# Attention with unnormalized probabilities: the sums of a pair inverted together and multiplied into the gate

## The chip, the core and the metric

The kernel runs on one core of a Trainium2 chip. The metric is the device time of one execution in microseconds. It is launched as one program, and its inputs and outputs lie in the chip's memory (DRAM here).

## What is computed

A trunk of two layers for 2048 frames of 1024 channels. Layer A is a gated mixing layer with a spatial gate. Layer B is attention in chunks of 64 frames: each chunk sees itself and the eight chunks before it. Only layer B matters here:

```python
q, z = jnp.split(h @ w_qz, 2, axis=-1)              # 16 heads of 64 channels
sc = jnp.einsum('bqhd,bkhd->bhqk', qc, kc) + bias   # relative-position bias
sc = jnp.where(valid, sc, NEG_INF)
p = jax.nn.softmax(sc, axis=-1)
o = jnp.einsum('bhqk,bkhd->bqhd', p, vc)
...
return (o * jax.nn.silu(z)) @ w_out
```

The softmax divides each row of exponentials by its sum. That division is linear in each row, so it can stand before the product with the values or after it.

## The kernel before, in words

All products are made in a split form: each matrix is held as a high part and a low part, and three matmuls (lines 113 to 115) give one product. Layer A and the values of layer B come first. The attention starts at about 1560 us and is one long loop, written out at build time.

**The loop.** The frames are cut into four blocks t of 512, and the 16 heads into eight pairs p. A pair holds eight units u: two heads times four groups of 128 queries. One pass of the loop (lines 1633 to 1669) works on one unit of one pair and interleaves several things:

- `score` for the unit two places ahead. PE multiplies queries and keys (L1320), 640 keys for a group. DVE adds the bias, negates, and finds the row minimum (L1328). ACT takes the exponential and sums each row into `sl` (L1335). DVE inverts that sum (L1338), and POOL multiplies the 128x640 probabilities `pr` by it (L1339).
- `flip` for this unit. PE transposes the five 128x128 squares of `pr` into PSUM (L1359). There is one such buffer, `tp`. ACT copies the high part out (L1362) and DVE makes the low part (L1363).
- `value` at every second unit. PE multiplies transposed probabilities and values for two groups (L1380 to L1387). ACT and DVE bring the result into `og32` (L1399 to L1406). At a pair's last group, which is reached at unit 0 of the next pair, DVE multiplies `og32` by 0.5 and the gate `Z` (L1413), and SP stores the product in DRAM (L1418) for the output projection. In the last block the pairs 6 and 7 skip the DRAM: `last_og` multiplies into the place where the output projection reads (L1486), and POOL makes the sums that it needs.
- Between these stand steps of other work (`ahead`): the projections of the next pair (matmuls `pj`) to queries, keys and the gate `Z`, and the output projection of the block before (matmuls `bo`). `SHARE` says how many steps of it each pair takes. In the last block's last pair little is left to fill in, and the last output projection follows behind the loop.

**Weights.** Each projection loads its weights (L208 or L210), ACT casts them to the high part (L199), and DVE makes the low part (L200). In block t=0 they are raw, so POOL scales them first (L184) and SP stores the scaled ones (L212) for the later blocks. In t=0, pairs 2 and 4 also make combinations of the output weights (`o_sums`).

**Queues and order.** Every DMA is issued by SP, in order: a DMA whose data or place isn't ready holds those behind it. Each engine also works in order. The tile framework lays out the order of each engine ahead of time from its own estimates, under the dependencies and some ordering edges (`paced_by_pj`), so it isn't strictly that of the source.

**What the change touches.** `score` (L1305), `flip` (L1344), the end of `value` (L1409 to L1418), the loop body (L1646 to L1666) and the end (L1670). The tile `og` (two buffers) and the gate `Z` (two buffers) get new users.

Of the kernel before, what the change touches and what calls it, by code (L numbers as in the profile page):

```python
# [9 lines left out]
F32 = mybir.dt.float32  # L10
# [3 lines left out]
ALU = mybir.AluOpType  # L14
# [19 lines left out]
def trunk_kernel(  # L34
# [41 lines left out]
    xtd = [[dram.tile([P, D], F32, name=f"xtd{t}_{b}") for b in range(TB)] for t in range(NT)]  # L76
    ogd = [dram.tile([P, 2, NPAIR, 2, P], F32, name=f"ogd{t}") for t in range(NT)]
    x2d = [[dram.tile([P, D], F32, name=f"x2d{t}_{b}") for b in range(TB)] for t in range(NT - 1)]

    reld = [dram.tile([P * 768], F32, name=f"reld{h}") for h in range(NH)]  # L80

# [1125 lines left out]
    with ExitStack() as bctx:  # L1207
# [81 lines left out]
        ogt = {}  # L1289
        bias_t = {}  # L1290
        prs = {}
        pts = {}
        og32s = {}

# [10 lines left out]
        def score(t, p, u):  # L1305

            hd, qb = divmod(u, 4)
            h = 2 * p + hd
            if qb == 1 and (h + 1 < NH or t + 1 < NT):
                load_bias(t + (h + 1) // NH, (h + 1) % NH)  # L1310
            bias = bias_t[t, h]
            kx = kt[t, p, hd]
            c0 = 0 if t > 0 else 512 - qb * P
            n = 640 - c0
            koff = qb * P + c0
            ps = pss.tile([P, 2, 512], F32, tag="ss", name=f"s{t}_{h}_{qb}")
            nseg, w = (2, 320) if n == 640 else (1, n)
            for i, q in enumerate(qt[t, p, hd]):
                for sg in range(nseg):
                    mm(  # L1320
                        ps[:, sg, :w], q[:, qb * P : (qb + 1) * P],
                        kx[:, koff + sg * w : koff + (sg + 1) * w],
                        start=i == 0, stop=i == 1,
                    )
            pr = sb.tile([P, 640], F32, tag="Pr", name=f"pr{t}_{h}_{qb}", bufs=4)
            nm = sm.tile([P, 1], F32, tag="nm", name=f"nm{t}_{h}_{qb}", bufs=4)
            sl = sm.tile([P, 1], F32, tag="sl", name=f"sl{t}_{h}_{qb}", bufs=4)
            nc.vector.tensor_tensor_reduce(  # L1328
                out=pr[:, c0:].rearrange("p (a b) -> p a b", a=nseg),
                in0=ps[:, :nseg, :w],  # L1330
                in1=bias[:, c0:].rearrange("p (a b) -> p a b", a=nseg),
                scale=-1.0, scalar=3.0e38, op0=ALU.add, op1=ALU.min,
                accum_out=nm[:],
            )
            nc.scalar.activation(  # L1335
                pr[:, c0:], pr[:, c0:], AF.Exp, scale=-1.0, bias=nm[:], accum_out=sl[:]
            )
            nc.vector.reciprocal(sl[:], sl[:])  # L1338
            nc.gpsimd.tensor_scalar(  # L1339
                pr[:, c0:], pr[:, c0:], sl[:], 1.0, op0=ALU.mult, op1=ALU.mult  # L1340
            )
            prs[t, h, qb] = pr

        def flip(t, p, u):  # L1344

            hd, qb = divmod(u, 4)
            h = 2 * p + hd
            g, qq = divmod(qb, 2)
            if qq == 0:
                pt = sb.tile([P, 2, 6, 256], F32R, tag="PT", name=f"pt{t}_{h}_{g}", bufs=2)  # L1350
                if t == 0:
                    nc.gpsimd.memset(pt[:, :, 5, 0:P].bitcast(F32), 0.0)
                pts[t, h, g] = pt
            pt = pts[t, h, g]
            pr = prs[t, h, qb]
            b0 = 0 if t > 0 else 4 - qb
            tp = ptr.tile([P, KD, P], F32, tag="tr", name=f"tp{t}_{h}_{qb}")
            for b in range(b0, 5):
                tpose(tp[:, b, :], pr[:, b * P : (b + 1) * P], ident[:])  # L1359
            cs = slice(qq * P, (qq + 1) * P)  # L1360
            oh = pt[:, 0, b0 + qq : 5 + qq, cs]
            nc.scalar.copy(oh, tp[:, b0:5, :])  # L1362
            nc.vector.tensor_tensor(  # L1363
                pt[:, 1, b0 + qq : 5 + qq, cs], tp[:, b0:5, :], oh.bitcast(F32), op=ALU.subtract
            )

        def value(t, p, hd, g):

            h = 2 * p + hd
            pt = pts[t, h, g]  # L1370
            po = pmm.tile([P, 2, 256], F32, tag="mm", name=f"pv{t}_{h}_{g}")
            hs = slice(hd * P, hd * P + P)

            def keys(i):
                return vtl[t, p][:, 2 * g + i, hs]

            if t > 0:
                mm(po[:, :, 0:P], keys(0), pt[:, :, 0, 0:P], start=True, stop=False)  # L1380
                mm(po[:, :, P:256], keys(5), pt[:, :, 5, P:256], start=False, stop=False)
                blocks = range(1, 5)
            else:
                blocks = range(4 - 2 * g, 6)
            for j in range(2):
                for i in blocks:
                    mm(  # L1387
                        po[:, 0, :], keys(i), pt[:, j, i, :],
                        start=(t == 0 and j == 0 and i == blocks[0]),
                        stop=(j == 1 and i == blocks[-1]),  # L1390
                    )
            if hd == 0 and g == 0:
                og32s[t, p] = sb.tile([P, T], F32, tag="og32", name=f"og32_{t}_{p}", bufs=1)
            og32 = og32s[t, p]
            r, r2 = halves(hd)
            ot = sb.tile([P, 2, 256], F32, tag="ot", name=f"ot{t}_{h}_{g}", bufs=1)
            oq = og32[r, g * 256 : (g + 1) * 256]
            n = 2 if t > 0 else 1
            nc.scalar.copy(ot[r, :n, :], po[r2, :n, :])  # L1399
            o1 = ot[r, :, :] if t > 0 else oq  # L1400
            nc.vector.tensor_tensor(
                o1, po[r, :n, :] if t > 0 else po[r, 0, :],
                ot[r, :n, :] if t > 0 else ot[r, 0, :], op=ALU.add,
            )
            if t > 0:
                nc.vector.tensor_tensor(oq, ot[r, 0, :], ot[r, 1, :], op=ALU.add)  # L1406
            if g == 0:
                return
            if hd == 1 and t + 1 == NT and p >= 6:  # L1409
                last_og(p, og32, zt[t, p])  # L1410
            elif hd == 1:
                og = sb.tile([P, T], F32, tag="og", name=f"og{t}_{p}", bufs=2)
                nc.vector.scalar_tensor_tensor(  # L1413
                    og[:], og32[:], 0.5, zt[t, p][:], op0=ALU.mult, op1=ALU.mult
                )
                o4 = og[:].rearrange("p (j r s) -> p r j s", j=2, r=2)
                for r_ in range(2):
                    nc.sync.dma_start(ogd[t][:, r_, p], o4[:, r_])  # L1418
# [214 lines left out]
        for t in range(NT):  # L1633
            for p in range(NPAIR):
# [11 lines left out]
                for u in range(8):  # L1646
# [9 lines left out]
                        finals.pop(0)()  # L1656
                    if todo:
                        todo.pop(0)()
                    if u % 2 == 0:
                        if u:  # L1660
                            value(t, p, *divmod(u // 2 - 1, 2))
# [6 lines left out]
                    run(gen)  # L1668
                before = t, p
        value(*before, 1, 1)  # L1670
        run(gen)
        while finals:
            finals.pop(0)()
# [58 lines left out]
```

## Time and profile before

| what | us |
|---|---|
| median of 3 runs (2724.27 to 2734.33) | 2726.85 |
| profiled execution | 2731.61 |
| its span | 2728.6 |
| PE matmul busy | 2630.1 |
| DVE busy | 1961.0 |
| ACT busy | 1324.8 |
| POOL busy | 909.8 |

The profile is one execution. PE is TensorE's matmuls and PEld its weight loads, which overlap them; DVE is VectorE, ACT ScalarE, POOL GpSimd, SP SyncE. A group row gives line, engine, operation, what it writes and reads, and its count; then busy time and the mean of one in ns; then the idle time just before it and what ended that. A wait row reads "who waited, for whom: us in total, times, longest". Busy matmuls overlap each other in the records: what PE spends on one is read from the distance between two starts.

### The profile page before, as it was taken

The numbers are of one execution on the slowest core, as the hardware profiler recorded it, in microseconds if no ns is written. First come the engines' busy times: TensorE is split into PE (matmuls) and PEld (weight loads), VectorE is DVE, ScalarE is ACT, GpSimd is POOL, SyncE is SP. The second block draws the span as 40 slices with busy tenths as digits, with TensorE's granted clock in tenths as the row PEclk, the third lists the DMA queues.
The fourth block names the chain that finished last, engine by engine and source line by source line (L and its number), as shares of the span: only waits on it lengthen the run. The fifth ranks groups of instructions, "written<-read, shape, count | busy, mean of one in ns | idle before, by whom it ended". The sixth has DMA issues, their size and how long they took to land. (4 is left out here: it accounts for less than half of the span.)

```text
span 2728.6 us, 38857 instructions
## 1 busy us (share of the span) xinstructions
PE 2630.1 (96%) x13216; PEld 2199.9 (81%) x13216; DVE 1961.0 (72%) x3097; ACT 1324.8 (49%) x2360; POOL 909.8 (33%) x906
## 2 busy tenths in 40 slices
PE   8999999999999999999989998999999999999997
PEld 7888888888888888888867776778887888788885
DVE  5655676676676669666677776677788778877787
ACT  5422242433424445332455465566656666666554
POOL 3512236142251414115143344322333223323243
PEclk9999999999999999999999999899999999999999
DMA  7899999989888879668667787766777667865567
GB/s 297 314 326 335 345 358 327 329 306 349 333 300 295 302 263 342 236 236 308 239 219 277 238 274 249 243 211 208 234 253 246 219 211 238 264 203 192 185 228 251
DMA packets 274773, 735.56 MB, mean 270 GB/s; under 512 B 29584, under 2 KB 61328, under 8 KB 274576
## 3 DMA queue, kind: packets, MB, share of 16 engines
q1 hardware_dynamic: 274576, 733.09, 77.9%
q8 instruction: 105, 1.72, 0.3%
q14 instruction: 92, 0.75, 0.1%
HBM read 540.56 MB, written 181.93 MB: 265 GB/s over the span
## 5 line engine op out<-in xcount | busy, mean ns | idle before, releaser
L113 PE MATMUL P<-T,S 128*128 128x512 f32 x1248 | 496.1, 398 | 2.7 <-ACT S L376 2.0
L115 PE MATMUL P<-T,S 128*128 128x512 f32 x1248 | 490.3, 393 | 0.0
L114 PE MATMUL P<-T,S 128*128 128x512 f32 x1248 | 489.1, 392 | 1.1 <-DVE T L379 1.1
L1339 POOL TENSOR_SCALAR pr<-pr,sl 128x640 f32<-128x640 f32 (+4 forms) x256 | 202.8, 792 | 553.9 <-DVE sl L1338 512.8
L113 PE MATMUL pj<-hh_b,wh_b 128*128 128x512 f32 x768 | 316.8, 412 | 7.7 <-ACT wh_b L199 6.7
L114 PE MATMUL pj<-hl_b,wh_b 128*128 128x512 f32 x768 | 307.4, 400 | 0.0
L115 PE MATMUL pj<-hh_b,wl_b 128*128 128x512 f32 x768 | 306.5, 399 | 0.0
L1335 ACT ACTIVATE pr<-pr,nm 128x640 f32<-128x640 f32 (+4 forms) x256 | 195.3, 763 | 222.4 <-DVE nm L1328 217.5
L115 PEld LDWEIGHTS P<-T,S 128*128 128x128 f32 x1248 | 235.4, 189 | 50.3
L113 PEld LDWEIGHTS P<-T,S 128*128 128x128 f32 x1248 | 235.9, 189 | 48.1 <-ACT S L376 2.3
L114 PEld LDWEIGHTS P<-T,S 128*128 128x128 f32 x1248 | 235.8, 189 | 46.9 <-DVE T L379 1.3
L1363 DVE TENSOR_TENSOR pt<-tp,pt 128x640 fp32r<-128x640 f32 (+4 forms) x256 | 188.8, 738 | 75.4 <-ACT pt L1362 73.1
L1328 DVE CUSTOM_DVE_ANT_0 pr<-s,bias 128x640 f32<-128x640 f32 (+4 forms) x256 | 188.2, 735 | 21.4 <-PE s L1320 15.6
L1362 ACT CAST pt<-tp 128x640 fp32r<-128x640 f32 (+4 forms) x256 | 158.6, 620 | 60.8 <-PE tp L1359 58.0
L1359 PEld LDWEIGHTS tp<-ident,pr 128*128 128x128 f32 x1120 | 135.1, 140 | 54.5 <-POOL pr L1339 15.9
L1359 PE MATMUL tp<-ident,pr 128*128 128x128 f32 x1120 | 165.8, 274 | 12.7 <-DVE pt L1363 6.5
L115 PEld LDWEIGHTS pj<-hh_b,wl_b 128*128 128x128 f32 x768 | 147.3, 192 | 32.6
L113 PEld LDWEIGHTS pj<-hh_b,wh_b 128*128 128x128 f32 x768 | 147.7, 192 | 27.5 <-ACT wh_b L199 8.3
L114 PEld LDWEIGHTS pj<-hl_b,wh_b 128*128 128x128 f32 x768 | 147.9, 193 | 17.3 <-issue 0.2
L1387 PE MATMUL pv<-pt,V 128*128 128x256 f32 x960 | 143.0, 289 | 11.2 <-ACT pt L1362 11.1
L200 DVE TENSOR_TENSOR wl_b<-raw_b,wh_b 128x1024 fp32r<-128x1024 f32 x96 | 122.9, 1280 | 42.4 <-ACT wh_b L199 41.2
L1387 PEld LDWEIGHTS pv<-pt,V 128*128 128x128 f32 x960 | 127.5, 193 | 14.9 <-ACT pt L1362 13.6
(291 smaller groups left out, 5941.5 us busy)
## 6 DMA issues: line engine op xcount, KB each, us to landing
S<-hsd SPq DMA_DIRECT2D x288, 512.0 KB, 5.5
rw<-in_w_a SPq DMA_DIRECT2D x108, 512.0 KB, 6.5
A<-ytd SPq DMA_DIRECT2D x72, 512.0 KB, 5.5
raw_b<-wk SPq DMA_DIRECT2D x72, 512.0 KB, 3.8
hsd<-S SPq DMA_DIRECT2D x56, 512.0 KB, 4.3
V<-vhd SPq DMA_DIRECT2D x56, 512.0 KB, 5.0
wh_bo<-ows SPq DMA_DIRECT2D x50, 512.0 KB, 4.5
wl_bo<-ows SPq DMA_DIRECT2D x50, 512.0 KB, 5.6
```

The source lines that it names most:

```text
L113: first = mm(ps, lh, rh, start=first, stop=False)
L114: mm(ps, lh, rl, start=False, stop=False)
L115: mm(ps, ll, rh, start=False, stop=last)
L200: tv(wl[:], raw[:], wh[:].bitcast(F32), op=sub)
L1328: nc.vector.tensor_tensor_reduce(out=pr[:, c0:].rearrange("p (a b) -> p a b", a=nseg), in0=ps[:, :nseg, :w], in1=bias[:, c0:].rearrange("p ...
L1335: nc.scalar.activation(pr[:, c0:], pr[:, c0:], AF.Exp, scale=-1.0, bias=nm[:], accum_out=sl[:])
L1339: nc.gpsimd.tensor_scalar(pr[:, c0:], pr[:, c0:], sl[:], 1.0, op0=ALU.mult, op1=ALU.mult)
L1359: tpose(tp[:, b, :], pr[:, b * P : (b + 1) * P], ident[:])
L1362: nc.scalar.copy(oh, tp[:, b0:5, :])
L1363: nc.vector.tensor_tensor(pt[:, 1, b0 + qq : 5 + qq, cs], tp[:, b0:5, :], oh.bitcast(F32), op=ALU.subtract)
L1387: mm(po[:, 0, :], keys(i), pt[:, j, i, :], start=(t == 0 and j == 0 and i == blocks[0]), stop=(j == 1 and i == blocks[-1]),)
```

## The change

The probabilities stay unnormalized: the reciprocal and POOL's multiplication for each unit go. The row sums of a pair's eight units are collected as the eight columns of one tile. At unit 6 (unit 5 in the very last pair) PE transposes that tile into a free place of the `tp` buffer, DVE inverts the 8x128 result, SP stores it in DRAM as a row, and SP loads it back so that each head's 512 reciprocals stand on 64 partitions. POOL multiplies this tile by the gate. The product with the output moves from unit 0 to unit 1 of the next pair and reads the new tile instead of `Z`.

```diff
+    rcd = [dram.tile([NPAIR, 8 * P], F32, name=f"rcd{t}") for t in range(NT)]
...
-            sl = sm.tile([P, 1], F32, tag="sl", name=f"sl{t}_{h}_{qb}", bufs=4)
+            if u == 0:
+                sums[t, p] = sm.tile([P, 8], F32, tag="sl", name=f"sl{t}_{p}", bufs=2)
...
-                pr[:, c0:], pr[:, c0:], AF.Exp, scale=-1.0, bias=nm[:], accum_out=sl[:]
-            )
-            nc.vector.reciprocal(sl[:], sl[:])
-            nc.gpsimd.tensor_scalar(
-                pr[:, c0:], pr[:, c0:], sl[:], 1.0, op0=ALU.mult, op1=ALU.mult
+                pr[:, c0:], pr[:, c0:], AF.Exp, scale=-1.0, bias=nm[:],
+                accum_out=sums[t, p][:, u : u + 1],
             )
...
+            if u == sums_at(t, p):
+                tpose(tp[0:8, 5, :], sums[t, p][:], ident[:])
...
+            if u == sums_at(t, p):
+                inverse(t, p, tp[0:8, 5, :])
+
+        def sums_at(t, p):
+            return 5 if t + 1 == NT and p + 1 == NPAIR else 6
+
+        def inverse(t, p, src):
+
+            rc = sm.tile([8, P], F32, tag="rc", name=f"rc{t}_{p}", bufs=1)
+            nc.vector.reciprocal(rc[:], src)
+            nc.sync.dma_start(rcd[t][p].rearrange("(a b) -> a b", b=P), rc[:])
+            w = zt[t, p, 1] = sb.tile([P, T], F32, tag="og", name=f"w{t}_{p}", bufs=2)
+            for hd in range(2):
+                nc.sync.dma_start(
+                    w[hd * 64 : hd * 64 + 64, :],
+                    rcd[t][p, hd * T : hd * T + T].partition_broadcast(64),
+                )
+            tg(w[:], w[:], zt[t, p][:], op=ALU.mult)
...
-            if hd == 1 and t + 1 == NT and p >= 6:
-                last_og(p, og32, zt[t, p])
-            elif hd == 1:
-                og = sb.tile([P, T], F32, tag="og", name=f"og{t}_{p}", bufs=2)
+        def gated(t, p):
+
+            og32, og = og32s[t, p], zt[t, p, 1]
+            if t + 1 == NT and p >= 6:
+                last_og(p, og32, og)
+            else:
                 nc.vector.scalar_tensor_tensor(
-                    og[:], og32[:], 0.5, zt[t, p][:], op0=ALU.mult, op1=ALU.mult
+                    og[:], og32[:], 0.5, og[:], op0=ALU.mult, op1=ALU.mult
                 )
...
+                    if u == 1 and before:
+                        gated(*before)
...
         value(*before, 1, 1)
+        gated(*before)
```

More of the change, by code (lines that the diff above doesn't have):

```diff
@@ L1291, in trunk_kernel @@
         prs = {}
+        sums = {}
         pts = {}
@@ L1406, in value @@
                 nc.vector.tensor_tensor(oq, ot[r, 0, :], ot[r, 1, :], op=ALU.add)
-            if g == 0:
-                return
-            if hd == 1 and t + 1 == NT and p >= 6:
-                last_og(p, og32, zt[t, p])
-            elif hd == 1:
-                og = sb.tile([P, T], F32, tag="og", name=f"og{t}_{p}", bufs=2)
+        def gated(t, p):
[3 more added lines that the diff above has]
+            else:
                 nc.vector.scalar_tensor_tensor(
-                    og[:], og32[:], 0.5, zt[t, p][:], op0=ALU.mult, op1=ALU.mult
+                    og[:], og32[:], 0.5, og[:], op0=ALU.mult, op1=ALU.mult
                 )
```

## The prediction

> **What bounds the kernel now.** I read the page first, then the busy time by stage, the chain of waits, the waits of each engine, and last the order of instructions inside single pairs.
>
> ```profile
> PE 2630.1 (96%) x13216; PEld 2199.9 (81%) x13216; DVE 1961.0 (72%) x3097; ACT 1324.8 (49%) x2360; POOL 909.8 (33%) x906
> ```
>
> ```profile
> 1560.00:1800.00 240.00, 211.56 (x1054) 171.66 (x1052) 161.18 (x381) 138.33 (x311) 105.59 (x161) 0.94 0.77 248
> 1800.00:2600.00 800.00, 786.36 (x4492) 679.01 (x4492) 633.25 (x1180) 493.65 (x883) 238.76 (x318) 0.99 0.69 221
> 2600.00:2728.60 128.60, 106.38 (x548) 84.91 (x546) 101.44 (x174) 62.93 (x122) 56.77 (x56) 0.98 0.74 248
> ```
>
> The change touches only the attention, from about 1560 us on. These rows give each stretch's length and the busy time of PE, PEld, DVE, ACT and POOL, then the granted clock, the DMA share and the GB/s. Block t=0 (1560 to 1800) leaves PE idle for 240 - 211.56 = 28.4 us, at a clock of 0.94. Blocks t=1 to 3 (1800 to 2600) leave 13.6 us idle of 800. The end leaves 22.2 us. The middle is thus bound by PE, and almost nothing else can shorten it:
>
> ```profile
> 2169.48 0.95 PE pv L1387 x8
> ...
> 2205.52 0.95 PE pv L1387 x8
> ```
>
> These two pieces of the chain (start, length) are one pair apart: 36.04 us a pair, and the chain between them stays on PE. What an edit outside PE can win lies in t=0, at the changes of block, and at the end. This is what PE's weight loads waited for on the probabilities, in t=0, then in t=1 to 3, then at the end (us in total, times, longest):
>
> ```profile
> PEld tp L1359 <- POOL pr L1339: 7.6, 8, 3.6
> ```
>
> ```profile
> PEld tp L1359 <- POOL pr L1339: 6.7, 11, 1.2
> ```
>
> ```profile
> PEld tp L1359 <- POOL pr L1339: 1.6, 1, 1.6
> ```
>
> **What goes: 256 divisions on POOL and 256 reciprocals on DVE.**
>
> ```profile
> L1339 POOL TENSOR_SCALAR pr<-pr,sl 128x640 f32<-128x640 f32 (+4 forms) x256 | 202.8, 792 | 553.9 <-DVE sl L1338 512.8 <-PE pj L115 10.5 <-PE pv L1387 9.9
> ...
> L1338 DVE RECIPROCAL sl<-sl 128x1 f32<-128x1 f32 x256 | 40.9, 160 | 76.5 <-ACT pr L1335 74.6
> ...
> L1557 POOL TENSOR_TENSOR oc<-oc,ou 128x512 f32<-128x512 f32 x12 | 17.8, 1485 | 23.8 <-DVE sl L1338 12.4 <-DVE oc L1556 11.3
> ```
>
> That is 202.8 us off POOL and 40.9 us off DVE, which also stops sitting in front of a reciprocal for 74.6 us. In t=1 to 3 this is off the path, and only the transposition's own wait counts. Of its 6.7 us, what is late next is the single transposition buffer, for which PE already waits on DVE's copy:
>
> ```profile
> PE tp L1359 <- DVE pt L1363: 2.7, 5, 0.9
> ```
>
> So I take 6.7 - 2.7 = **-4.0 us** there (bounds 0 and -6.7). At the end I take -1.0 of the 1.6.
>
> In t=0 there is more. POOL also scales the weights there (L184), and it works in order:
>
> ```profile
> POOL pr L1339 <- DVE sl L1338: 87.2, 51, 4.4
> ...
> POOL raw_b L184 <- DMA raw_b<-in_w_kqz: 8.4, 3, 3.6
> ```
>
> ```profile
> ACT wh_b L199 <- POOL raw_b L184: 20.0, 8, 5.0
> ```
>
> ```profile
> 1575.93 1.04 POOL L1339 TENSOR_SCALAR pr<-pr,sl 128x512 f32<-128x512 f32 x2 [3.62 <-DVE sl L1338]
> 1576.91 0.32 POOL L1352 MEMSET pt<- 128x256 f32 x1
> 1577.18 1.91 POOL L184 TENSOR_TENSOR raw_b<-raw_b,bg 128x1024 f32<-128x1024 f32 x1
> ```
>
> POOL stood for 87.2 us of t=0 in front of a division that waited for its reciprocal, and in the last rows a scaling stood behind 3.62 us of such a wait. ACT, in order as well, waited 20.0 us for scalings. Of these 8.4 us are POOL itself waiting for the weights' load, so at most 20.0 - 8.4 = 11.6 us are owed to the divisions. With the transposition's 7.6 us the ceiling is 19.2 us. I take **-8 us**, about two fifths, since once the division is gone the load or the single transposition buffer is often late at the same place (bounds 0 and -19.2).
>
> **What is added on PE: 32 transpositions of the sums.** The rows of five transpositions and the next matmuls:
>
> ```profile
> 2218.68 0.71 PE L1359 MATMUL tp<-ident,pr 128*128 128x128 f32 x5
> 2219.14 0.48 PE L113 MATMUL pj<-hh_b,wh_b 128*128 128x512 f32 x1
> 2219.46 0.40 PE L114 MATMUL pj<-hl_b,wh_b 128*128 128x512 f32 x1
> ```
>
> Five take 0.46 us of issue time, 0.55 us with the slower first matmul behind them: 0.11 us each. The new one joins five others, so I take this. It counts in the 24 full pairs: 24 x 0.11 = **+2.6 us**. Bounds: 24 x 0.46 / 5 = 2.2, and 32 times a fifth of the row's 0.71 us, 4.5. The eight in t=0 fall into idle time. If that were filled, they would cost 0.9 more.
>
> A transposition of sums needs the exponential of unit 7 at unit 6's place. In a full pair:
>
> ```profile
> 2228.21 0.19 ACT L1335 ACTIVATION_READ_ACCUMULATOR pr<-pr,nm 128x1 f32 x1
> ```
>
> ```profile
> 2231.60 0.71 PE L1359 MATMUL tp<-ident,pr 128*128 128x128 f32 x5
> ```
>
> The sum of unit 7 is there at 2228.40, and the sixth transposition would come at 2232.06: 3.7 us of cover, so no new wait. In the last pair it sits at unit 5, without this cover. I count that within the end's 1.0.
>
> **What is added on DVE, POOL and the queues.** DVE gets 32 reciprocals over 8x128. With one element a partition a reciprocal takes 160 ns, and the copies of 640 elements below take 0.82 us, so I put one of 128 elements between 0.16 and 0.82 us, at most 26 us in total against 40.9 + 74.6 removed. POOL gets 32 multiplications of 128x512 at about 1485 ns (L1557): 47.5 us for 202.8. The product with the output keeps its instruction, one unit later. Nothing of this is on PE's path while its chain is on time:
>
> ```profile
> 2233.62 0.82 DVE L1363 TENSOR_TENSOR pt<-tp,pt 128x640 fp32r<-128x640 f32 x1 [0.41 <-ACT pt L1362]
> ...
> 2249.50 0.83 DVE L1363 TENSOR_TENSOR pt<-tp,pt 128x640 fp32r<-128x640 f32 x1 [0.41 <-ACT pt L1362]
> ```
>
> The first row is unit 6's copy, behind which the reciprocal comes. The second is unit 1's copy in the next pair, behind which the output's product (DVE) will wait for POOL. Between their ends lie 15.9 us. The chain in it: reciprocal up to 0.8, store of 4 KB, load of 2 x 128 KB, product 1.5. For store and load the nearest row is a store followed by a load of the same data, on the chain at a change of block:
>
> ```profile
> 2053.77 3.01 DMA x2d<-ou
> 2056.78 0.02 issue
> 2056.80 4.15 DMA y<-x2d
> ```
>
> 7.2 us for larger pieces, so 9.5 us in all, with 6.4 us of cover. If that were gone, DVE would stand, and behind the product stand the next pair's score rows and copies, for which PE waits.
>
> The wait that I do count is SP's. All these transfers go through SP in order. The 32 stores wait for a reciprocal, and the 64 loads wait until the store has landed, while the loads of weights stand behind. In t=1 to 3 I count zero, because PE's own 36 us a pair hide it: the chain between the two pieces of a full pair never leaves PE for a load. If that cover went, it would be up to a store's landing for each of 24 pairs, 24 x 2.8 = 67 us. In t=0 it is otherwise. The chain there:
>
> ```profile
> 1630.39 0.46 SPq L1418
> ...
> 1630.90 5.11 DMA raw_b<-in_w_kqz
> ...
> 1636.15 1.91 POOL raw_b L184
> ```
>
> A load of weights went out right behind the output's store (L1418), and PE's chain ran through load and scaling. The stores there land in:
>
> ```profile
> ogd<-og SPq DMA_DIRECT2D x14, 128.0 KB, 2.8
> ```
>
> SP stands for 2.8 us in a pair of 30 us with three weight loads. The chance that one comes due meanwhile is 3 x 2.8 / 30 = 0.28, and it is held 1.4 us on the mean. That gives 8 x 0.28 x 1.4 = **+3 us** (bounds 0, and the whole 8 x 2.8 = 22.4).
>
> Sum: -4.0 - 1.0 - 8 + 2.6 + 3 = **-7.4 us**. The profiled execution took 2731.61 us (span 2728.6), 4.8 over the median of 2726.85. It would be 2724.2, and the median of runs **2719.4 us**, 0.27% less. About 0.5% (13.6 us) is what a measurement of this kernel can tell from no change, so this counts as "the same".
>
> **Rivals.** *Faster: t=0 comes free.* The terms take their full size (-6.7, -1.6, -19.2) and SP's costs nothing: with +2.6 this is -24.9, so 2702 us. For it: POOL's 87.2 us of waiting, and the clock of 0.94, which rises where gaps close. Against: DMA is 0.77 busy in t=0, and the chain just shown runs through a load, not a division.
>
> *Slower: SP's wait for the landed store decides t=0.* If the loads of weights are due when SP stands, each pair of t=0 loses the 2.8 us (22.4), and since the weights then come late, POOL's freedom there is worth nothing: 22.4 + 2.6 - 4.0 - 1.0 = +20, so 2747 us. It decides from the point where a weight load's slack in the queue is under a store's landing. For it: the chain above, where the slack was nothing. Against: the order in the queue is laid out ahead, so a load that is due earlier can stand in front.
> The Trainium skill ("DMA: Bandwidth & Descriptors", section "Two DMAs through the same engine are not ordered") speaks for this rival: a load that depends on a store may be issued only after the issuing engine has waited for the store's completion. The trace agrees in the pair of transfers at 2053.77 and 2056.80. The same page ("Anatomy of one DMA") puts the fixed part of a DMA, for another issuing path, at about 2.0 us. By it the eight waits would be an estimated 16 us, and the rival would stand at 2740.
>
> *Nothing but the transpositions:* the waits on POOL go, and others end at the same moment. Then +2.6, so 2729.5 us.
>
> **How the numbers follow.** Forecast 0.40, nothing but the transpositions 0.12, faster rival 0.24, slower rival 0.24. The rivals lie beyond 0.5% and the other two within, so faster by over 0.5% has 0.24, within 0.5% has 0.52, slower has 0.24. The range runs from the faster rival's 2702 to the slower one's 2747, with about a tenth left out beyond each. The forecast's own range goes from the middle's full term with SP's wait free (-6.7 - 1.0 - 8 + 2.2, 2713) to t=0 giving nothing with PE's dear end (-4.0 - 1.0 + 4.5 + 3, 2729).
>
> **What would show it.** Right: a full pair of 36.1 to 36.2 us in t=1 to 3; no waits of PE on POOL's product; ACT's 20.0 us for scalings down to some 12; the t=0 stretch about 5 us shorter. Wrong: SP rows in t=0 where a weight load follows the loads of reciprocals with a gap and ACT's wait for scalings grows (slower rival); t=0 shorter by 15 us and a clock near 1 (faster rival); DVE idle in front of the output's product, which would mean that the 6.4 us of cover is not there; or a full pair over 36.5 us, which no term explains.

## The result and the profile after

The changed kernel takes 2748.95 us (median of 6 runs, 2745.03 to 2758.86), the kernel before 2729.64 beside it: a ratio of 1.0075, 95% interval 1.0052 to 1.0097. A second measurement gave 2749.82 and a ratio of 1.0082 (1.0066 to 1.0098). So it is slower by some 20 us, where I had forecast 7 us less; the time lies 2 us beyond the upper end of my range. The profile of the changed kernel fell on the longest of its runs (2758.86 us, span 2757.1), so I show its lines but take sizes from the medians, or from two profiles (the second took 2755.22 us). Line numbers have moved: the copies of the transposed probabilities are now L1364 (ACT, high part) and L1365 (DVE, low part), the sums' transposition is L1361, the reciprocal L1377, its store L1378, the loads L1381, POOL's product L1385, the product with the output L1434.

The page's busy times, and the stretches of the prediction (length, then PE, PEld, DVE, ACT, POOL, granted clock, DMA share, GB/s):

```profile
PE 2649.3 (96%) x13248; PEld 2208.8 (80%) x13248; DVE 1964.4 (71%) x2873; ACT 1325.6 (48%) x2360; POOL 752.5 (27%) x682
```

```profile
1560.00:1800.00 240.00, 212.54 (x1038) 169.58 (x1037) 156.95 (x316) 133.85 (x302) 77.97 (x102) 0.94 0.78 252
1800.00:2600.00 800.00, 779.50 (x4435) 670.05 (x4433) 627.78 (x1010) 487.05 (x873) 118.83 (x161) 0.99 0.71 227
2600.00:2757.10 157.10, 129.27 (x660) 102.88 (x658) 119.41 (x185) 75.64 (x143) 47.85 (x47) 0.96 0.68 224
```

POOL lost 157 us of work, and nothing came of it. In the middle PE now stands idle for 800 - 779.50 = 20.5 us, where it was 13.6. PE's busy time rose by 19 us, though its added work is 32 short transpositions: the same matmuls took longer. Both are explained below. In fixed stretches two kernels do different work, so this table counts from the first copy of a block's probabilities (`pt<-tp` on ACT) to the next block's (us, one profile each; the last column is an experiment):

| stretch | before | changed | changed, again | no inverse |
|---|---|---|---|---|
| up to t=0 | 1571.3 | 1572.0 | 1572.4 | 1567.8 |
| t=0 | 233.6 | 239.6 | 242.3 | 224.4 |
| t=1 | 294.7 | 300.5 | 299.0 | 294.4 |
| t=2 | 294.1 | 299.8 | 297.1 | 291.1 |
| t=3, p0 to p6 | 250.0 | 250.7 | 250.1 | 250.2 |
| last pair and end | 84.9 | 94.4 | 92.5 | 83.7 |

The loss is in t=0, in t=1 and t=2, and at the end. What I had foreseen is there too. ACT's wait for scalings in 1560 to 1800 fell from 20.0 us (us in total, times, longest):

```profile
ACT wh_b L200 <- POOL raw_b L185: 11.1, 8, 4.3
```

The chain of the reciprocals ended in time. Here it is in a full pair, on DVE, SP, POOL and DVE (start, length):

```profile
2247.06 0.94 DVE L1377 RECIPROCAL rc<-tp 8x128 f32<-8x128 f32 x1
```

```profile
2248.03 0.28 SPq L1378 DMA_DIRECT2D rcd<-rc  x1
2251.26 1.11 SPq L1381 DMA_DIRECT2D w<-rcd  x2
```

```profile
2255.05 1.30 POOL L1385 TENSOR_TENSOR w<-w,Z 128x512 f32<-128x512 f32 x1 [1.47 <-DMA w<-rcd]
```

```profile
2259.86 0.69 DVE L1434 SCALAR_TENSOR_TENSOR w<-og,w 128x512 f32<-128x512 f32 x1
```

From the reciprocal's start (2247.06) to the end of POOL's product (2256.35) it takes 9.3 us, against 9.5 in the prediction. DVE's product starts at 2259.86, so 3.5 us of cover are left: the room is 12.8 us, and not the 15.9 of the prediction, as DVE's product now stands ahead of unit 1's copy. But PE's waits for DVE's copy out of the single transposition buffer grew in 1800 to 2600 from 2.7 us (5 times, longest 0.9):

```profile
PE tp L1359 <- DVE pt L1365: 10.4, 11, 2.8
```

**One place, read through.** In pair p7 of t=1, SP stores the reciprocals, and then stands before it may load them (rows of SP, then DVE, then PE, of the changed kernel):

```profile
2063.47 0.28 SPq L1378 DMA_DIRECT2D rcd<-rc  x1
2064.92 0.33 SPq L1541 DMA_DIRECT2D x2d<-ou  x1
2067.96 1.11 SPq L1381 DMA_DIRECT2D w<-rcd  x2
2069.16 0.54 SPq L1557 DMA_DIRECT2D y<-x2d  x1
```

```profile
2070.36 2.35 DVE L170 TENSOR_TENSOR hl_b<-xr_b,hh_b 128x1024 fp32r<-128x1024 f32 x2
2074.74 1.41 DVE L1560 SCALAR_TENSOR_TENSOR y<-y,rr_f,gf 128x512 f32<-128x512 f32 x2 [2.03 <-POOL w L1385]
2076.07 0.82 DVE L1365 TENSOR_TENSOR pt<-tp,pt 128x640 fp32r<-128x640 f32 x1
```

```profile
2073.72 0.40 PE L115 MATMUL pj<-hl_b,wh_b 128*128 128x512 f32 x1
2076.94 0.77 PE L1359 MATMUL tp<-ident,pr 128*128 128x128 f32 x5 [2.82 <-DVE pt L1365]
2077.46 0.36 PE L1400 MATMUL pv<-pt,V 128*128 128x256 f32 x1
2078.53 0.65 PE L1322 MATMUL s<-K,Qh 128*128 128x320 f32 x2 [0.70 <-DVE nm L1331]
...
2080.42 0.79 PE L114 MATMUL pj<-hh_b,wh_b 128*128 128x512 f32 x1 [0.71 <-ACT wh_b L200]
2081.01 0.63 PE L116 MATMUL pj<-hh_b,wl_b 128*128 128x512 f32 x1
2081.44 0.63 PE L114 MATMUL pj<-hh_b,wh_b 128*128 128x512 f32 x1
...
2085.28 0.58 PE L114 MATMUL pj<-hh_b,wh_b 128*128 128x512 f32 x1
2085.70 0.39 PE L115 MATMUL pj<-hl_b,wh_b 128*128 128x512 f32 x1
2085.93 0.40 PE L116 MATMUL pj<-hh_b,wl_b 128*128 128x512 f32 x1
```

The load of `y` (an output row) went out at 2069.16. It reads what the store at 2064.92 wrote, and by the trace's semaphores that had landed at 2068.29; so SP's wait for the reciprocals' store and their two loads held it back by 0.9 us. DVE, in order, stood 2.03 us for `y`: the row names POOL's product, but the semaphore of `y`'s own load was complete at 2074.65, 5.5 us after it went out. The copy that frees the transposition buffer stood behind `y`, and PE waited 2.82 us. In the kernel before the copy stands ahead of the same step (DVE):

```profile
2060.13 0.82 DVE L1363 TENSOR_TENSOR pt<-tp,pt 128x640 fp32r<-128x640 f32 x1
2062.04 1.78 DVE L1539 SCALAR_TENSOR_TENSOR y<-y,rr_f,gf 128x512 f32<-128x512 f32 x2 [1.10 <-issue]
```

Then comes what I had not priced at all: from 2081.01 to 2085.28 the matmuls of 128x512 last 0.63 us and follow each other every 0.43 us, and at 2085.70 they are back at 0.39 us and 0.23. The granted clock had halved (0.50 from 2080 to 2084). These 4.7 us of slow matmuls (11 of them, with 0.20 us too much each) cost another 2.1 us. But this is not all a loss against the kernel before, which waits at the same change of block for something else and has its half clock too (PE):

```profile
2065.54 0.56 PE L1320 MATMUL s<-K,Qh 128*128 128x320 f32 x2 [2.39 <-DVE nm L1328]
2068.41 0.80 PE L113 MATMUL pj<-hh_b,wh_b 128*128 128x512 f32 x1 [2.01 <-ACT wh_b L199]
2069.00 0.63 PE L115 MATMUL pj<-hh_b,wl_b 128*128 128x512 f32 x1
```

The pair takes 41.8 us in the changed kernel, 40.3 in the kernel before and 36.9 without the inverse. So the place shows how a wait and the clock add up; against the kernel before the change lost 1.5 us here, and without the inverse the place is 3.5 us shorter.

I counted such stretches in the record of the granted clock, from the first copy of t=0 to the last matmul: 7 with 37.5 us in the profile before, 8 with 54.6 us in the changed kernel's, 3 with 13.7 us in that without the inverse. Each lasts 3.4 us or 6.8, once 10.2. At 0.427 in the place of 0.232 us a step, up to 46% of a stretch is lost. The Trainium skill ("TensorE: Matmul & The Clock Gate", section "What's actually happening") has a gate that passes the full clock or half of it, by TensorE's activity in windows of about 3.4 us that run freely. The trace agrees in the two clocks (1.00 and 0.50) and in the lengths (3.4 us and multiples of it).

### The profile page after: what moved, and what is told of

It is laid out like the page before. It is cut to its first block, busy times and chain, and to the rows that moved or that the text cites. A ratio compares the mean times of both kernels' runs of the same rounds, so it can differ in the third digit from the quotient of the medians.

```text
span 2757.1 us, 38242 instructions
## 1 busy us (share of the span) xinstructions
PE 2649.3 (96%) x13248; PEld 2208.8 (80%) x13248; DVE 1964.4 (71%) x2873; ACT 1325.6 (48%) x2360; POOL 752.5 (27%) x682
## 2 busy tenths in 40 slices
DMA packets 280401, 744.05 MB, mean 270 GB/s; under 512 B 30864, under 2 KB 62864, under 8 KB 280208
## 3 DMA queue, kind: packets, MB, share of 16 engines
q1 hardware_dynamic: 280208, 741.61, 78.6%
## 5 line engine op out<-in xcount | busy, mean ns | idle before, releaser
L1365 DVE TENSOR_TENSOR pt<-tp,pt 128x640 fp32r<-128x640 f32 (+4 forms) x256 | 189.0, 738 | 153.8 <-ACT pt L1364 152.1
L1364 ACT CAST pt<-tp 128x640 fp32r<-128x640 f32 (+4 forms) x256 | 158.7, 620 | 90.1 <-PE tp L1359 81.5
L116 PEld LDWEIGHTS pj<-hh_b,wl_b 128*128 128x128 f32 x768 | 147.3, 192 | 40.3 <-DVE wl_b L201 8.0
L114 PEld LDWEIGHTS pj<-hh_b,wh_b 128*128 128x128 f32 x768 | 148.1, 193 | 31.8 <-ACT wh_b L200 12.6
L1303 POOL MEMSET bias<- 64x64 f32 x64 | 9.3, 145 | 527.4 <-DMA bias<-reld 413.3
L201 DVE TENSOR_TENSOR wl_b<-raw_b,wh_b 128x1024 fp32r<-128x1024 f32 x96 | 131.0, 1364 | 29.8 <-ACT wh_b L200 28.9
```

The costliest lines, as they stand in the source:

```text
L114: first = mm(ps, lh, rh, start=first, stop=False)
L116: mm(ps, ll, rh, start=False, stop=last)
L201: tv(wl[:], raw[:], wh[:].bitcast(F32), op=sub)
L1303: nc.gpsimd.memset(bias[0:64, 576:640], NEG)
L1365: nc.vector.tensor_tensor(pt[:, 1, b0 + qq : 5 + qq, cs], tp[:, b0:5, :], oh.bitcast(F32), op=ALU.subtract)
```

## The experiments

Every run lists its span and mean granted clock, so each mean span can be split: span times clock is its length at full clock, waits included, and the rest is lost to the clock. For the kernel before this is 2693 + 34 us (the means beside the different groups are 2692 to 2693, and 32 to 35). Not all that is called lost costs time: in the profile before the clock is at 0.50 from 2722.8 us to the end, behind the last matmul, and that alone counts as 2.9 us. All diffs are against the changed kernel unless another is named. The groups ran at different times and on different chips, and the kernel before beside them has medians from 2726.8 to 2729.4 us. So a difference between medians of two groups of less than some 3 us means little.

| kernel | median us | ratio to before, 95% | full clock + lost |
|---|---|---|---|
| no inverse (e1) | 2714.2 | 0.9940 (0.9922 to 0.9959) | 2687.9 + 24.9 |
| + reciprocal (g2) | 2716.8 | 0.9963 (0.9950 to 0.9977) | 2687.0 + 28.5 |
| + 15 transpositions (i3) | 2719.5 | 0.9967 (0.9956 to 0.9979) | 2689.8 + 28.1 |
| + DMAs (f2) | 2722.2 | 0.9981 (0.9967 to 0.9994) | 2693.7 + 27.4 |
| before, product moved (k1) | 2723.1 | 0.9980 (0.9967 to 0.9993) | 2690.7 + 31.2 |
| + transposition at unit 7 (i2) | 2728.2 | 0.9998 (0.9985 to 1.0010) | 2695.2 + 31.8 |
| + transposition (g1) | 2729.5 | 1.0006 (0.9995 to 1.0017) | 2694.5 + 32.3 |
| + transposition, reciprocal (f1) | 2732.0 | 1.0013 (1.0004 to 1.0023) | 2698.2 + 32.1 |
| all, cheaper parts (h2) | 2743.8 | 1.0053 (1.0040 to 1.0067) | 2705.9 + 37.9 |
| loads late (f4) | 2744.1 | 1.0063 (1.0045 to 1.0080) | 2699.5 + 43.9 |
| all, on ACT's queue (h1) | 2745.0 | 1.0068 (1.0054 to 1.0082) | 2708.0 + 36.1 |
| reciprocal first (e3) | 2745.1 | 1.0051 (1.0035 to 1.0067) | 2704.1 + 38.4 |
| no product (e4) | 2747.8 | 1.0056 (1.0035 to 1.0077) | 2708.3 + 36.1 |
| changed (again, g0) | 2749.8 | 1.0082 (1.0066 to 1.0098) | 2707.7 + 40.3 |
| no landing (e2) | 2760.1 | 1.0105 (1.0083 to 1.0127) | 2712.5 + 45.2 |
| POOL's queue (f3) | 2774.7 | 1.0177 (1.0158 to 1.0197) | 2727.0 + 47.7 |
| stored by elements (j1) | 2961.7 | 1.0854 (1.0838 to 1.0870) | 2831.0 + 128.8 |
| the same on ACT (j3) | 3040.3 | 1.1161 (1.1137 to 1.1185) | 2876.1 + 166.1 |

**First group: which part.** My theory was that the added chain costs the time. Its rivals were the parts of it, and the removal itself.

No inverse (e1):

```
-            if u == sums_at(t, p):
-                tpose(tp[0:8, 5, :], sums[t, p][:], ident[:])
...
-            if u == sums_at(t, p):
-                inverse(t, p, tp[0:8, 5, :])
...
-                    og[:], og32[:], 0.5, og[:], op0=ALU.mult, op1=ALU.mult
+                    og[:], og32[:], 0.5, zt[t, p][:], op0=ALU.mult, op1=ALU.mult
```

> The change's removal alone: the probabilities stay unnormalized and nothing takes the division's place. The transposition of the sums, the reciprocal of 8x128, its store, the two loads and POOL's product are left out, and the product with the gate stays at unit 1 of the next pair, so the output lacks the division. Three theories share the loss of some 19 us among the added work: the round trip through SP's queue (A), the reciprocal of 0.94 us on VectorE which holds the transposition tile (B), POOL's product beside VectorE (C). All three expect 2715 to 2725 us here, as my forecast's gains without its costs. A fourth (D) says that taking the division out lays the engines' instructions out in a worse order, whatever is added: 2740 to 2750 us.

2714.2 us. The fourth theory falls: what goes brings 13.6 us, as forecast, and what is added costs 35. The views of the cores of before, of the changed kernel and of this one:

```profile
core 0: 2728.6 us, clock 0.986
```

```profile
core 0: 2757.1 us, clock 0.983
```

```profile
core 0: 2711.6 us, clock 0.992
```

At full clock these two, before and without the inverse, are 2690 us alike in the profiles (2728.6 x 0.986, 2711.6 x 0.992). By all runs 5 us of the gain are work and waits, and 9.6 the clock. Of the 17.0 us between the two profiles, 3.5 lie ahead of the attention, in code that both share (the table's first row), so a part of such a difference is of the run and not of the change.

No landing (e2), `rc0` being stored once ahead of the stage:

```
-                    rcd[t][p, hd * T : hd * T + T].partition_broadcast(64),
+                    rc0[0, hd * T : hd * T + T].partition_broadcast(64),
```

> The changed kernel, but the two loads read a row in DRAM that is written once ahead of the stage; the store of the reciprocals still runs, and nobody reads it. The division is by a constant, so the output is another. SP then never waits for a store to land. A (SP's wait delays what stands behind it in the queue, the output's row and the weights above all): about 2733 us, and the wait of TensorE in front of the second transpositions of the pairs p7 (3.0 and 1.8 us in t=1 and t=2) is under 1 us. B, C and D: 2745 to 2750 us, with those waits as they are.

2760.1 us: slower than the changed kernel. SP's wait for the store's landing, my slower rival, is not the price by itself. This kernel's orders are others too (its loads wait for no store, so they stand elsewhere in SP's queue), and t=0 grew to 244.7 us in its profile. Why it is slower by 10 us stays open, and with it what the landing costs.

Reciprocal first (e3):

```
+                nc.vector.reciprocal(sums[t, p][:], sums[t, p][:])
                 tpose(tp[0:8, 5, :], sums[t, p][:], ident[:])
...
-            nc.vector.reciprocal(rc[:], src)
+            nc.scalar.copy(rc[:], src)
```

> The changed kernel with the reciprocal taken of the sums as they stand, 128x8, ahead of their transposition; ScalarE copies the transposed 8x128 out of PSUM. VectorE's 0.94 us of a pair become about 0.2, and the transposition tile is let go by ScalarE's copy. B (VectorE's reciprocal costs): about 2735 us. A, C and D: 2744 to 2750 us.

2745.1 us, some 4 less than the changed kernel, with overlapping intervals: not the main price.

No product (e4):

```
-            tg(w[:], w[:], zt[t, p][:], op=ALU.mult)
```

> The changed kernel without POOL's product of the loaded rows and the gate: the rows go straight into VectorE's product, so the gate is left out of the output. TensorE's order of instructions stays exactly that of the changed kernel. C (POOL's 32 products of 1.3 to 2.0 us lengthen VectorE's splits of the weights beside them and make its product wait): about 2738 us, and the waits of TensorE on the split of the weights in front of the pairs p5 (1.3 and 1.5 us) go. A, B and D: 2745 to 2750 us.

2747.8 us: POOL's products cost 1 to 2 us or nothing.

**Second group: one half alone.** Taking parts away from the whole had shown little, so I put halves on top of the kernel without the inverse. The transposition and the reciprocal (f1) are the changed kernel's lines without the store, the loads and the product.

> The kernel without the inverse (2714.2 us) with two parts put back: the transposition of the sums and VectorE's reciprocal out of PSUM. Nothing is stored, loaded or multiplied, so the output lacks the division. Q (the work on TensorE and VectorE is the price: 32 x 0.11 us of transposition, 32 x 0.94 us of reciprocal with the transposition tile held): 2732 to 2740 us. P (the three DMAs of a pair in SP's one queue are the price): 2716 to 2722 us.

2732.0 us, 17.8 more, at the lower edge of Q's range.

The DMAs alone (f2), in the place of `rc` a tile written once, in the place of the gate its rows:

```
-            nc.vector.reciprocal(rc[:], src)
-            nc.sync.dma_start(rcd[t][p].rearrange("(a b) -> a b", b=P), rc[:])
+            nc.sync.dma_start(rcd[t][p].rearrange("(a b) -> a b", b=P), src[:])
...
-            tg(w[:], w[:], zt[t, p][:], op=ALU.mult)
```

> The kernel without the inverse (2714.2 us) with the other half put back: at the same place SP stores a constant tile of 8x128, loads it as rows twice, and VectorE's product takes these rows in the place of the gate. No transposition, no reciprocal, no product on POOL; gate and division are missing from the output. P (three DMAs of a pair in SP's queue, the loads waiting for the store to land): 2735 to 2745 us. Q: 2716 to 2724 us.

2722.2 us, 8.0 more, within Q's range and far from P's. In the profiles t=0 alone is longer by 10.7 us (235.1 for 224.4), and the other stretches by -2.2 to +1.1. POOL's wait for the weights' loads within t=0, from the waits of the kernel without the inverse and then of that with the DMAs:

```profile
POOL raw_b L185 <- DMA raw_b<-in_w_kqz: 19.0, 7, 6.4
```

```profile
POOL raw_b L185 <- DMA raw_b<-in_w_kqz: 27.9, 8, 6.6
```

So three more transfers a pair cost 8 us or so in t=0 and nothing where PE has 36 us a pair to hide them. That they cost it by delaying the weights in SP's queue is likely from these two rows (8.9 us more), but not shown: in the changed kernel, with the same transfers and a longer t=0, the same wait is 14.4 us, less than without the inverse. The halves add up to 25.8 of the 35 us; the other 9 arise when they stand together, and I could not place them.

POOL's queue (f3): the store and the loads by `nc.gpsimd` in the place of `nc.sync`.

> The changed kernel, but POOL and not SP issues the store of the reciprocals and the two loads, so that no weight load and no output row stands behind them. P: 2722 to 2735 us, the wait of the second transpositions of p7 (3.0 and 1.8 us) gone, and t=0 shorter than the changed kernel's 239.6 us by 8 or more. Q: 2744 to 2752 us. R (the chain is too long for its place, and VectorE waits for its end): 2745 to 2760 us, as a wait on POOL delays POOL's other work too.

2774.7 us: the mechanism is R's, but the time is 15 us beyond R's range. DVE now waits 15.9 us in t=0 for POOL's product (4 times, up to 5.7), and what stands behind it in order waits with it.

Loads late (f4):

```
             nc.sync.dma_start(rcd[t][p].rearrange("(a b) -> a b", b=P), rc[:])
+
+        def fetch(t, p):
+
             w = zt[t, p, 1] = sb.tile([P, T], F32, tag="og", name=f"w{t}_{p}", bufs=2)
...
+                    if u == 0 and before:
+                        fetch(*before)
                     flip(t, p, u)
```

> The changed kernel with the two loads and POOL's product moved from unit 6 to unit 0 of the next pair, some 10 us later, when the store of the reciprocals has landed. SP's wait for the landing (35.9 us in 26 times) goes, but two loads and a product have only the 5 us up to VectorE's product at unit 1. P by its wait for the landing: 2735 to 2742 us. P by its mere DMAs, and Q: 2745 to 2752 us. R: 2755 us or more.

2744.1 us, between the ranges of P and Q and 5 less than the changed kernel. In its profile t=0 is shorter (234.2 us for 239.6 and 242.3). The last pair, which has no next one to hide its loads, takes 32.5 us from its first copy of probabilities to its last, for 26.9 and 27.6 in the two profiles of the changed kernel.

**Third group: transposition or reciprocal.** The changed kernel again (g0):

> The changed kernel itself once more, beside the kernels of this group: its first profile fell on the longest of its six runs (2758.9 us against a median of 2749.0). All theories: 2743 to 2753 us.

2749.8 us. The transposition alone (g1) and the reciprocal alone (g2), each on the kernel without the inverse:

```
+            if u == sums_at(t, p):
+                tpose(tp[0:8, 5, :], sums[t, p][:], ident[:])
```

> The kernel without the inverse (2714.2 us) with the transposition of the sums alone put back, read by nobody; the division is left out. With the reciprocal it stood at 2732.0 us. Q1 (the 17.8 us are VectorE's reciprocal, 0.94 us in front of the next rows of VectorE's order): 2717 to 2720 us, the 32 x 0.11 us on TensorE. Q2 (they are the transposition, which waits for the sums of the eighth unit and stands in TensorE's order): 2726 to 2732 us.

```
+            if u == sums_at(t, p):
+                nc.vector.reciprocal(rc[:], rc[:])
```

> The kernel without the inverse (2714.2 us) with a reciprocal of 8x128 alone put back at the same place, of a constant tile in SBUF, so that it waits for nothing and holds no transposition tile; the division is left out. Q1 by VectorE's time: 2724 to 2732 us. Q1 by the hold of the transposition tile alone: 2714 to 2719 us. Q2: 2714 to 2718 us.

2729.5 and 2716.8 us: Q2. The reciprocal, which I had come to suspect, costs 2.6 us, and 32 transpositions, 3.5 us of TensorE's time, cost 15.3. By the ratios to the kernel before beside each, the transposition costs 18 us, the DMAs 11 and the reciprocal 6, the last with an interval that overlaps that of the kernel without the inverse; so the ranking of the three is the same. By the mean spans of the table (14.0 us apart) 6.6 us of the transposition are work and waits, and 7.4 the clock. Within t=1, t=2 and t=3 the profile with the transposition falls behind by 0.8, 1.2 and 0.7 us over the six pairs p0 to p5, 0.1 to 0.2 a pair. Of the 18.3 us between the two profiles, 3.7 lie ahead of the attention, 4.1 in t=0, and most of the rest in p6, p7 and the change of block. In the matmul rows of the two traces TensorE's order in p1 to p4 of t=1 to t=3 is the same but for the transposition and at most three rows a pair; at the changes of block and in t=0 matmuls have changed places. The wait for the sums themselves is 0.4 us, once.

All, on ACT's queue (h1): e3 and f4 together, the last pair's loads at its unit 7, the DMAs by `nc.scalar`.

> The whole division in another form: reciprocals of the sums as they stand (128x8), the transposed rows copied out by ScalarE, the store and the loads issued by ScalarE and not by SP, the loads and POOL's product at unit 0 of the next pair, when the store has landed (for the last pair at unit 7). If the price of the changed kernel is VectorE's 0.94 us (Q1) and the DMAs in SP's queue (P, 8 us, nearly all in t=0): 2718 to 2727 us, faster than both kernels. If any added instruction in this place moves the engines' orders as much (D'): 2738 to 2750 us.

2745.0 us: D'. DVE waits 9.8 us in t=0 for POOL's product.

**Last groups: why a transposition costs 15 us.** The same at unit 7 (i2):

```
-            return 5 if t + 1 == NT and p + 1 == NPAIR else 6
+            return 7
```

> The kernel without the inverse (2714.2 us) with the transposition of the sums alone put back, as in the run of 2729.5 us, but at unit 7 of the pair in the place of unit 6; the division is left out. The work is the same. If the price lies in the place that it takes in the engines' orders (O): another time, 2716 to 2722 us. If it is the transposition's own work and wait, wherever it stands (W): 2727 to 2732 us.

2728.2 us: the total stays (W), which speaks against the place in the order as the price. But it falls elsewhere: t=1 is 2.2 us shorter than without the inverse, t=0 9.2 longer.

The product's move alone (k1): the kernel before with `gated` at unit 1 of the next pair, dividing as before.

> The kernel before with one part of the change alone: VectorE's product with the gate, and its stores, moved from the end of a pair to unit 1 of the next. The division stays as before. If the gain of 13.6 us of the kernel without the inverse is the division's removal: 2724 to 2731 us. If it is this move: 2714 to 2720 us.

2723.1 us, between both: of the 13.6 us, about 6 are this move, which I had priced at nothing, and 7 to 9 the division's removal (13.6 - 6.4, or 2723.1 - 2714.2). It is faster than both kernels, by 0.2%, but less than what I can tell from no change in one measurement.

The division without TensorE (j1), and its DMAs on ACT's queue (j3), both with loads as in h1:

```
+            nc.vector.reciprocal(src[:], src[:])
+            nc.sync.dma_start(rcd[t][p].rearrange("(a b) -> b a", b=P), src[:])
```

> The whole division without TensorE: reciprocals of the sums as they stand (128x8), stored by SP straight into rows in pieces of four bytes, loaded at unit 0 of the next pair (for the last pair at unit 7) and multiplied by POOL. By the parts measured so far, 2714.2 us without the inverse and 8.0 us for the DMAs on SP: 2719 to 2726 us, faster than the kernel before. If the store in pieces of four bytes lands too late for the loads, or the orders come out as badly as with the transposition (O): 2730 to 2745 us.

> The same with ScalarE issuing the store and the loads. If the 8.0 us of the DMAs are SP's queue in t=0: 2715 to 2721 us, and t=0 near the 224 us of the kernel without the inverse. If they are what the DMAs wait for and what waits for them, on whichever queue: 2722 to 2735 us, with ScalarE's waits in the place of SP's.

2961.7 and 3040.3 us. A store of 4 KB in pieces of four bytes lands after 10.7 us, and SP stood for it:

```profile
rcd<-sl SPq DMA_DIRECT2D x32, 4.0 KB, 10.7
```

```profile
SPq L1381 <- DMA rcd<-sl: 274.2, 30, 11.0
```

Both lie far outside all that was expected, and say nothing on the transposition. The question went to 15 pairs in which the order mostly stays (i3):

```
-            if u == sums_at(t, p):
+            if u == sums_at(t, p) and t and p < 5:
                 tpose(tp[0:8, 5, :], sums[t, p][:], ident[:])
```

> The kernel without the inverse (2714.2 us) with the transposition of the sums put back in the 15 pairs p0 to p4 of t=1 to t=3 alone; the division is left out. TensorE's order is that of the kernel without the inverse but for these 15. C (the transposition costs its 0.11 us where TensorE is never idle; the rest arises in t=0 and in the last pairs of a block, by other orders, waits and a halved clock): 2714 to 2718 us, at a mean granted clock of 0.990 or more. W (each transposition costs its 15.3 / 32 us): 2720 to 2724 us.

2719.5 us, between the two expectations. At full clock it adds 1.9 us, 0.13 for each of 15, nearer to C's 1.7 than to the 3.1 that W's share of the 6.6 us would be; 3.2 more go to the clock. The pairs' lengths say it more clearly: against the profile without the inverse 13 of the 15 pairs are longer by at most 0.15 us (median 0.11), where W needs 0.48 in each; two are longer by 0.37 and 1.14. And t=0, here without transpositions, takes 224.5 us, as without the inverse; with them it took 228.5 and, at unit 7, 233.6. In its profile one slow stretch of 3.5 us stands in p6 of t=2, where there is none without the inverse, and 6.0 us were lost ahead of the attention, in code that both share. So the clock's part of such a sum varies with the run, and the time alone does not exclude W; the pairs do, for the full pairs. Why the transpositions cost as much in t=0 and around the changes of block stays open: the orders differ there, but no run shows that the order is the reason.

All, cheaper parts (h2): h1 with the DMAs on SP.

> The whole division with reciprocals of the sums as they stand, the transposed rows copied by ScalarE, loads and POOL's product at unit 0 of the next pair (for the last pair at unit 7), and all DMAs on SP: the run of 2745.0 us with SP's queue in the place of ScalarE's. If parts add up (2714.2, 15.3 for the transposition, 8.0 for the DMAs, about 1 for the reciprocals): 2736 to 2741 us. If the late loads in SP's queue cost less than at unit 6: 2729 to 2735 us. If ScalarE's queue was the better place: 2746 to 2755 us.

2743.8 us, above the sum of the parts (2736 to 2741) and below the range of the third guess. No form of the division after the product came near the kernel before.

## Why the prediction was wrong

- *What goes, -13.0 us.* Right in sum: -13.6. By the stretches of the profile without the inverse: t=0 -9.2 (forecast -8), t=1 to t=3 p6 -3.1 (forecast -4.0), the end -1.2 (forecast -1.0). But some 6 of it belong to the product's move, which I took as free, and some 9.6 of the 14.9 us between the mean spans is clock, which the sum did not have.
- *The transpositions, +2.6, at most 4.5.* **This step failed most**: +15.3. The price of 0.11 us holds in the full pairs (0.11 to 0.13), and the sums themselves are waited for in time (0.4 us, once). What failed is that one full pair was carried to all 32: "the eight in t=0 fall into idle time" is wrong by 4 to 9 us, and at the changes of block more is lost. There TensorE's order came out another way too; that this is the reason is my reading, not shown. Even of the full pairs of t=1 and t=2, which I gave 36.1 to 36.2 us, only one (p2 of t=2, 36.23) came out so; p1 took 36.7 in t=1 and t=2, and p4 39.3 for 36.8. In p4 it is the reciprocal and POOL's product: with the reciprocal ahead of the transposition (e3) it takes 36.9, without the product (e4) 38.4. My sign "a full pair over 36.5 us" was badly chosen, for in the kernel before p3 takes 38.1 and p4 36.8.
- *DVE's reciprocals, nothing on the path.* 0.94 us each, over my upper bound of 0.82. Alone +2.6, on top of the transposition 2.5, both within what groups differ by; but it stands on the path in p4 and, with the transposition, at the end.
- *SP's wait in t=0, +3 (0 to 22.4).* The DMAs alone cost 8.0, nearly all in t=0: mis-sized, inside its bounds. Which wait it is stays open: with the landing taken away (e2) nothing was won, with the loads moved behind the landing (f4) 5 us were. The slower rival's 2747 us is near the measured time by luck: the runs do not bear out its sum (it wins 5.0 and adds 25.0, where 13.6 were won and 35 added). The rule that it took from the Trainium skill ("DMA: Bandwidth & Descriptors", section "Two DMAs through the same engine are not ordered") does hold in the trace: SP stood 2.95 us between the end of the store's issue at 2248.31 and the load at 2251.26.
- *The cover of the chain, 6.4 us.* The chain was right (9.3 us in place of 9.5), the room was not (12.8 in place of 15.9), so the cover was 3.5 us. It was enough: no idle DVE in front of the product but for 2.4 us in t=0.
- *A wait priced by its length.* The missing term. Every term of my sum was one for one; a stretch of waits beyond some 2.5 us also halves the clock behind it. Of the 20 to 23 us between the mean spans, 6 to 8 go to the clock by the split above.
- *The end, -1.0.* It became 7.6 to 9.5 us longer. In f1, without any DMA, it is already 6.7 longer than without the inverse, so that is the transposition and the reciprocal at unit 5, where I had seen that there is no cover and still counted it within the end's gain. It takes both: with the transposition alone the end is 83.5 us and with the reciprocal alone 82.8, for 83.7 without. In f1 TensorE's matmuls wait 5.8 us in the last pair for DVE's copies out of the transposition buffer, 0.6 with the transposition alone.

## What to carry to other kernels

Price an added instruction not in the steadiest stretch but at the places that already wait (the start of a stage, the change of block, the end), and ask there what moves when the order of the engines is laid out again. Where TensorE is the bound, add to each wait near 2 or 3 us the clock that it can take down, some 1.5 to 3 us more, and look whether the kernel before does not already pay it there. To find out what an edit costs, put its parts one by one on the kernel that lacks them all: taking single parts out of the whole showed 1 to 5 us each, or even a loss (e2), adding them showed 15, 8 and 3.

## What the runs showed of the hardware

- *The clock follows the waits.* In 16 profiles (all but j1, j3, i3 and h2) take each wait of TensorE over 0.5 us from the first copy of t=1 to that of the last pair, and sum the idle time of the 3.4 us up to its end. A stretch of granted clock 0.50 began within 3.4 us of that end in 4 of 115 cases with under 1.5 us, in 28 of 56 with 1.5 to 2.5 us, and in 22 of 22 with more. The Trainium skill ("TensorE: Matmul & The Clock Gate", section "What's actually happening") has the half clock after at least one idle window of about 3.4 us; here more than 2.5 us out of 3.4 were enough in each case.
- *It also makes the runs of one program differ.* The kernel before in this study: 20 runs at a mean clock of 0.986 have a mean span of 2728.7 us, 17 at 0.989 one of 2724.0.
- *A reciprocal goes by its length in a partition.* 8x128 takes 935 ns out of PSUM and 936 ns out of SBUF, 128x1 160 ns; the same 1024 elements as 128x8 take 203 ns (e3).
- *Pieces of four bytes.* The same 4 KB, stored as rows, held SP's load until 3.2 us behind the store's issue in the pair shown (2248.03) and 4.5 us in p7; as 1024 elements they land in 10.7 us; the profile counts 312976 packets on the queue for the changed kernel's 280208, which is 32 x 1024 more. The Trainium skill ("DMA: Bandwidth & Descriptors", section "Rules for kernel authors") says that a strided last dimension becomes one descriptor per element; the trace agrees.
- *POOL's product beside DVE.* The split of the weights takes 1280 ns on the mean before, 1364 in the changed kernel, 1308 without these products of POOL, and 2.33 us in this case beside two operations of POOL:

```profile
1990.59 2.33 DVE L201 TENSOR_TENSOR wl_b<-raw_b,wh_b 128x1024 fp32r<-128x1024 f32 x1
```

```profile
1990.21 1.61 POOL L1588 TENSOR_TENSOR ou<-ou,ou 128x512 f32<-128x512 f32 x1 [3.85 <-DVE ou L1587]
1992.10 1.96 POOL L1385 TENSOR_TENSOR w<-w,Z 128x512 f32<-128x512 f32 x1 [0.28 <-DMA w<-rcd]
```
